# A linear-recurrence layer: the first of two triangular inversions is issued beside the projections, the first half of the scan beside the second half's operands and inversion

## The chip, the cores and the metric

One core of one Trainium2 chip runs the whole kernel. The metric is the device time of one execution in microseconds; lower is better.

## The reference, cut to what matters

The reference is a two-layer diffusion backbone: layer 0 (retention, grouped attention, a dense feed-forward part), layer 1 (differential attention and a bidirectional RWKV-7 time mixing, then eight experts of which each token takes two). The change lies in RWKV-7 of layer 1: 8 heads of 64, 256 context tokens followed by 256 latent tokens, once forward (d = 0) and once backward (d = 1). Per token and head it computes

```
decay = exp(-exp(-softplus(-(w0[d] + tanh(wd) @ w2[d])) - 0.5))
a     = sigmoid(a0[d] + ad @ a2[d]);   kd = k * (1 + (a - 1) * k_a);   kk = k * k_k / |k * k_k|
s_new = s * decay + (s @ -kk) (kk * a)^T + v kd^T          # state, 64 x 64
y     = (s if d else s_new) @ r
```

Only the latent tokens' y is used; the context half gives the state with which the latent half begins.

## The kernel before, in words

The 512 tokens are two halves (half 0 is the context, half 1 the latent tokens), each half four chunks of 64 tokens. The recurrence is done in chunked form: inside a chunk, the effect of the state's own products is a unit lower triangular system of 64 rows, whose inverse is computed ahead for all chunks, heads and both directions at once. All names below are in `layer1`.

- `project` (L842): pairs of 128 projection columns, each weight chunk split into a high and a low part (`wsplit`, L261: ScalarE writes whi, VectorE wlo) and multiplied three times; `shift` (L832) mixes neighbouring tokens. It fills rT, kT, vT, twd, adT, sgd.
- `unit_keys` (L907): kk. `prep(d, half)` (L932): decays and operands of one direction and half. It loads w2, a2 and w0 on SyncE's queue (L900, L901, L245), makes sigmoids (L946, L955), cumulated decays by matmul (L965, L966), their exponentials (L967 to L969), and writes AR and BK (L971 to L981). Its work tiles Ei, Ee, En, at, tb have one buffer each.
- `inv_blocks(half)` (L1001): the 32x32 blocks, by matmul (L1017, L1020), into Lc and Lo; a 32x32 transposition gives M (L1027). `inv_diag(half)` (L1031): 31 elimination steps of two dependent VectorE instructions each (L1042, L1044) turn N into the blocks' inverses. `inv_join(half)` (L1049): two transpositions, two rounds of small matmuls (gp L1068, wp L1077) and copies (L1060, L1082) give XF, the inverses of 64 rows.
- `chain(half)` (L1194): the scan over four chunks, both directions side by side: `prepare` (L1109; the masks are L1119), `state_in`, `solve` (needs XF, L1155), `state_out`, and for half 1 `outputs`.

Program order before: a weave of projections 8, 10, 0, 2, 14 with unit_keys, prep(0,0), prep(1,0); inv_blocks(0); a weave of prep(0,1), prep(1,1), inv_blocks(1) with inv_diag(0); the bonus products (rk, L1089 to L1097); inv_join(0); a weave of chain(0) with inv_diag(1), inv_join(1); then chain(1) with `finish`.

`weave` (L94) sets only the order in which generators issue: each counts as done in so many steps, and the one least far along goes next. The tile framework then plans each engine's queue: an instruction that is ready by its estimates may go ahead of an earlier one that is not. On the chip each engine's queue runs in the planned order. PSUM has eight banks of 128x512; `banks` (L152) says which of them each use takes in turn, and a bank is one tile tag with one buffer. A tile that takes a closed pool's place waits for the tiles that lay there.

Of the kernel before, what the change touches and what calls it, by code (L numbers as in the profile page):

```python
# [105 lines left out]
def seq(*gens):  # L106
    for g in gens:
        yield from g
# [8 lines left out]
def drain(g):  # L117
    for _ in g:
        pass
# [9 lines left out]
def _build(top, tc, nc, V, S, G, T, I, O):  # L129
    cp = top.enter_context(tc.tile_pool(name="const", bufs=1))  # L130
    st = top.enter_context(tc.tile_pool(name="st", bufs=4))
    cur = {}
# [19 lines left out]
    def banks(**by_use):  # L152

        use.update(by_use)

    def bank(kind):
# [2 lines left out]
            n = use[kind][turn[kind] % len(use[kind])]  # L159
            return ps.tile([128, 512], F32, name=name, tag=f"b{n}")  # L160
        return take
    acc, tpp, att, ybank = (bank(k) for k in ("acc", "tp", "at", "y"))
    banks(acc=range(6), tp=(6, 7))
    cur["re"] = cur["ce"] = ExitStack()
    top.callback(lambda: [cur[k].close() for k in ("we", "xe", "me", "he", "re", "ce", "pe")])
# [630 lines left out]
    def layer1():  # L796
# [185 lines left out]
            yield  # L982

        operands(qA, 0)
        banks(at=(3, 4, 5))
        weave((seq(*(project(i) for i in (8, 10, 0, 2, 14))), 15), (seq(unit_keys(), prep(0, 0), prep(1, 0)), 20))
        for k in ("we", "xe", "he"):
            cur[k].close()
        eB = ExitStack()
        qB = eB.enter_context(tc.tile_pool(name="rwb", bufs=1, side="right", reuse_waits="tile"))  # L990
        operands(qB, 1)
        eI = ExitStack()
        qI = eI.enter_context(tc.tile_pool(name="rwi", bufs=1, side="right", reuse_waits="tile"))
        XF = [(qI, qB)[i].tile([128, 2, 4, 4, 64], F32, name=f"XF{i}") for i in range(2)]
        for half in range(2):
            G.memset(XF[half], 0.0)
        bn = lambda name: qI.tile([128, 32, 32], F32, name=name, tag="bn", bufs=5)
        flat = lambda x: x.rearrange("p a b -> p (a b)")
        iv = {}

        def inv_blocks(half):  # L1001

            Lc = bn("Lc")
            off = acc("off")
            for d in range(2):
                dg = acc("dg")
                for c in range(4):
                    for p in range(4):
                        cp_ = slice((c * 4 + p) * 32, (c * 4 + p) * 32 + 32)
                        for x in range(2):  # L1010
                            for h in range(2):
                                hs = slice(64 * h, 64 * h + 64)
                                A = lambda i: AR[d, half][hs, p, c, 32 * i:32 * i + 32]
                                B = lambda i: BK[d, half][hs, p, c, 0, 32 * i:32 * i + 32]
                                o_ = 64 * h + 32 * x
                                l_, r_ = (A(x), B(x)) if d == 0 else (B(x), A(x))
                                T.matmul(dg[o_:o_ + 32, cp_], l_, r_, start=True, stop=True,  # L1017
                                         tile_position=(64 * h, o_))
                                if x == d:
                                    T.matmul(off[o_:o_ + 32, cp_], B(d), A(1 - d), start=True, stop=True,  # L1020
                                             tile_position=(64 * h, o_))
                S.activation(flat(Lc[:, 16 * d:16 * d + 16]), dg, AF.Copy)
                yield
            Lo = qI.tile([128, 16, 32], F32, name="Lo", tag="Lo", bufs=1)
            S.activation(flat(Lo), off, AF.Copy)
            M = bn("M")
            V.transpose(M.rearrange("p r c -> p c r"), Lc.rearrange("p u c -> p c u"))  # L1027
            iv[half] = M, Lo
            yield
# [19 lines left out]
        def inv_join(half):  # L1049

            N, Lo = iv[half]
            X0, X1 = bn("X0"), bn("X1")
            V.transpose(X0.rearrange("p u c -> p c u"), N.rearrange("p r c -> p c r"))
            V.transpose(X1.rearrange("p u r -> p r u"), N)
            yield
            xf, xt = (X0, X1), (X1, X0)
            xF = XF[half].rearrange("p d c a t -> p d (c a) t")
            for d in range(2):
                for x in range(4):
                    (S.copy if x % 2 else V.tensor_copy)(xF[32 * x:32 * x + 32, d, :, 32 * (x % 2):32 * (x % 2) + 32],  # L1060
                                                         xt[d][32 * x:32 * x + 32, 16 * d:16 * d + 16])
            gp = acc("gp")
            Gs = qI.tile([128, 16, 32], F32, name="Gs", tag="Gs", bufs=1)
            for d in range(2):
                for u in range(16):
                    for h in range(2):
                        i_, o_ = 64 * h + 32 * d, 64 * h + 32 * (1 - d)
                        T.matmul(gp[o_:o_ + 32, u * 32:u * 32 + 32], Lo[i_:i_ + 32, u], xf[d][i_:i_ + 32, 16 * d + u],  # L1068
                                 start=True, stop=True, tile_position=(i_, o_))
            S.activation(flat(Gs), gp, AF.Copy)  # L1070
            yield
            wp_ = acc("wp")
            for d in range(2):
                for u in range(16):
                    for h in range(2):
                        o_, i_ = 64 * h + 32 * d, 64 * h + 32 * (1 - d)
                        T.matmul(wp_[o_:o_ + 32, u * 32:u * 32 + 32], Gs[i_:i_ + 32, u], xt[d][i_:i_ + 32, 16 * d + u],  # L1077
                                 start=True, stop=True, tile_position=(i_, o_))
            for d in range(2):
                for h in range(2):  # L1080
                    o_ = 64 * h + 32 * d
                    S.activation(xF[o_:o_ + 32, d, :, 32 * (1 - d):32 * (1 - d) + 32],  # L1082
                                 wp_[o_:o_ + 32].rearrange("p (u t) -> p u t", u=16), AF.Copy)
            yield

        banks(acc=(3, 4, 5), at=(0, 1, 2))
        drain(inv_blocks(0))
        weave((seq(prep(0, 1), prep(1, 1), inv_blocks(1)), 19), (inv_diag(0), 32))
        rk = q.tile([128, 4, 256], F32, name="rkT", tag="Ei", bufs=1)  # L1089
        for p in range(4):  # L1090
            V.scalar_tensor_tensor(rk[:, p], rT[:, p], vcol("rk", p), kT[:, p, 256:512], op0=ALU.mult, op1=ALU.mult)
        hind = rc("hind").rearrange("p (a b) -> p a b", a=4)
        for b in range(2):
            t = tpp()
            for p in range(4):
                T.matmul(t[:, 0:8], rk[:, p, b * 128:(b + 1) * 128], hind[:, p], start=(p == 0), stop=(p == 3))
            V.tensor_copy(bon[:, b], t[:, 0:8])  # L1097
        banks(acc=range(6))
        drain(inv_join(0))
        eT.close()  # L1100

        def chain_pool():
            return top_pool("chain")

        eC, q = chain_pool()
        St, Y, ops, zs = {}, {}, {}, {}
        heads = [(p, h, slice(64 * h, 64 * h + 64)) for p in range(4) for h in range(2)]

        def prepare(d, half, c):  # L1109

            bk, ar = BK[d, half], AR[d, half]
            gc, w = half * 4 + c, 64 * (1 + half)
            Lm = q.tile([128, 8, 128], F32, name="Lm", tag="Lm", bufs=4)
            a = [acc("lm") for h in range(2)]
            for p, h, hs in heads:
                T.matmul(a[h][:, p * w:(p + 1) * w], bk[hs, p, c].rearrange("p a t -> p (a t)"), ar[hs, p, c, 0:w],
# [4 lines left out]
            t = tpp()  # L1121
            for p in range(4):
                T.transpose(t[:, p * 128:(p + 1) * 128], bk[:, p, c].rearrange("p a t -> p (a t)"), ident)
            bkt = q.tile([128, 512], F32, name="bkt", tag="bkt", bufs=4)
            S.activation(bkt, t, AF.Copy)
            UV = q.tile([128, 512], F32, name="UV", tag="UV", bufs=4)
            G.memset(UV[0:64], 0.0)
            t = tpp()
            for p in range(4):
# [4 lines left out]
        def state_in(d):  # L1134

            c, ar, Lm, bkt, UV = ops[d]
            S0 = St.get(d)
            z = acc("z")
            zv = z[:, 0:256].rearrange("p (a v) -> p a v", a=4)
            for p, h, hs in heads:  # L1140
                hd = 2 * p + h
                T.matmul(zv[hs, p], Lm[:, 4 * h + p, 0:64], UV[:, hd * 64:hd * 64 + 64], start=(p == 0),
                         stop=(S0 is None and p == 3), tile_position=(0, 64 * h), skip_group_check=True)
            if S0 is not None:
                for p, h, hs in heads:
                    T.matmul(zv[hs, p], ar[hs, p, c, 0:64], S0[hs, p], start=False, stop=(p == 3),
                             tile_position=(64 * h, 64 * h), skip_group_check=True)
            zs[d] = q.tile([128, 4, 64], F32, name="zs", tag="zs", bufs=2)
            (S.copy if d else V.tensor_copy)(zs[d], zv)

        def solve(d, half):
# [68 lines left out]
                ops.update(nxt)  # L1220
                yield

        weave((chain(0), 16), (seq(inv_diag(1), inv_join(1)), 32))
        eI.close()
        eC.close()
        mh, ml = (qA.tile([128, 8, 256], F32R, name=n_, tag=t_) for n_, t_ in (("mixh", "BK00"), ("mixl", "BK10")))
        G1, G2 = (qA.tile([128, 2, 512], F32, name=n_, tag=t_) for n_, t_ in (("G1", "AR00"), ("G2", "AR10")))
        cur["sb"], cur["rb"] = 2, 5
# [15 lines left out]
        def finish():  # L1244

            for b in range(2):
# [14 lines left out]
                yield  # L1261
                split_next()
                yield
        eC, q = chain_pool()
        banks(acc=range(4), y=(4, 5))
        for h in range(2):
            Y[h] = ybank("Y")
# [621 lines left out]
```

## Time and profile before

| | us |
|---|---|
| median of 3 runs | 2106.11 (2105.66 to 2109.67) |
| profiled execution | 2111.12 |
| its span | 2109.4 |
| TensorE busy in the span | 2018.4 (96%) |
| VectorE | 1637.6 (78%) |
| ScalarE | 1214.5 (58%) |

PE is TensorE's matmul stream, PEld its weight loads, DVE VectorE, ACT ScalarE, POOL GpSimd, SP SyncE, which issues most transfers. A busy PE is not a PE at its peak. PEclk is the granted TensorE clock as a share of full speed (1.0 is 2.4 GHz, 0.5 is 1.2 GHz). "L1042" is a line of the kernel before; "out<-in" are tile names; the bracket behind a row is the engine's idle time ahead of it and what ended it. RWKV-7 and its inversions take about a tenth of the span; the expert stage takes the half behind it.

### The profile page before, as it was taken

The numbers are of one execution on the slowest core, as the hardware profiler recorded it, in microseconds if no ns is written. First come the engines' busy times: TensorE is split into PE (matmuls) and PEld (weight loads), VectorE is DVE, ScalarE is ACT, GpSimd is POOL, SyncE is SP. The second block draws the span as 40 slices with busy tenths as digits, with TensorE's granted clock in tenths as the row PEclk, the third lists the DMA queues.
The fourth block names the chain that finished last, engine by engine and source line by source line (L and its number), as shares of the span: only waits on it lengthen the run. The fifth ranks groups of instructions, "written<-read, shape, count | busy, mean of one in ns | idle before, by whom it ended". The sixth has DMA issues, their size and how long they took to land. (4 is left out here: it accounts for less than half of the span.)

```text
span 2109.4 us, 30113 instructions
## 1 busy us (share of the span) xinstructions
PE 2018.4 (96%) x11649; PEld 1620.8 (77%) x11650; DVE 1637.6 (78%) x2075; ACT 1214.5 (58%) x1563; POOL 93.4 (4%) x107
## 2 busy tenths in 40 slices
PE   6999989999999899889989999999999999999997
PEld 2766778878788677778878888888888888888885
DVE  3977794675557657678578999899989899899987
ACT  3643342222235445643348878777777777777775
POOL 0211010000000110100010000000000000000000
PEclk8999999999999999977899999999999999999999
DMA  8535352476545331101187989999999999999993
GB/s 301 165 102 168 104 177 70 136 240 215 182 159 190 113 90 55 34 19 36 38 324 269 366 312 365 342 355 378 345 352 344 357 383 349 345 360 356 372 366 134
DMA packets 224202, 494.00 MB, mean 234 GB/s; under 512 B 11355, under 2 KB 45262, under 8 KB 224054
## 3 DMA queue, kind: packets, MB, share of 16 engines
q1 hardware_dynamic: 219968, 482.62, 65.1%
q10 hardware_dynamic: 4086, 9.40, 1.3%
q8 instruction: 93, 1.52, 0.3%
q14 instruction: 55, 0.45, 0.1%
HBM read 490.87 MB, written 1.11 MB: 233 GB/s over the span
## 5 line engine op out<-in xcount | busy, mean ns | idle before, releaser
L278 DVE TENSOR_TENSOR mlo<-mraw,mhi 128x1024 fp32r<-128x1024 f32 x668 | 788.6, 1222 | 74.0 <-ACT mhi L277 57.0
L277 ACT ACTIVATE mhi<-mraw 128x1024 fp32r<-128x1024 f32 x668 | 684.3, 1058 | 98.8 <-PE y L274 48.2
L267 ACT ACTIVATE whi<-raw 128x1024 fp32r<-128x1024 f32 (+1 forms) x150 | 153.1, 1025 | 274.1 <-PE acc L274 113.0
L268 DVE TENSOR_TENSOR wlo<-raw,whi 128x1024 fp32r<-128x1024 f32 (+1 forms) x146 | 173.0, 1189 | 136.4 <-ACT whi L267 136.1
L272 PE MATMUL acc<-hTh,whi 128*128 128x512 f32 (+1 forms) x504 | 191.4, 382 | 0.0
L273 PE MATMUL acc<-hTl,whi 128*128 128x512 f32 (+1 forms) x504 | 187.6, 373 | 0.0
L274 PE MATMUL acc<-hTh,wlo 128*128 128x512 f32 (+1 forms) x504 | 186.7, 371 | 0.0
L342 DVE SCALAR_TENSOR_TENSOR part<-mraw,cond,part 128x1024 f32<-128x1024 f32 x112 | 150.0, 1360 | 40.5 <-DMA mraw<-in_mod_w 40.3
L273 PE MATMUL g<-mlo,xh 128*128 128x512 f32 x448 | 180.3, 402 | 0.0
L272 PE MATMUL g<-mhi,xh 128*128 128x512 f32 x448 | 176.7, 395 | 0.0
L273 PE MATMUL y<-mlo,acts 128*128 128x512 f32 x448 | 175.6, 392 | 0.3 <-DVE mlo L278 0.3
L274 PE MATMUL g<-mhi,xl 128*128 128x512 f32 x448 | 175.2, 391 | 0.0
L273 PE MATMUL u<-mlo,xh 128*128 128x512 f32 x448 | 174.8, 390 | 0.1
L272 PE MATMUL u<-mhi,xh 128*128 128x512 f32 x448 | 174.8, 390 | 0.0
L274 PE MATMUL y<-mhi,acts 128*128 128x512 f32 x448 | 174.8, 390 | 0.0
L274 PE MATMUL u<-mhi,xl 128*128 128x512 f32 x448 | 174.4, 389 | 0.0
L272 PE MATMUL y<-mhi,acts 128*128 128x512 f32 x448 | 151.4, 390 | 0.0
L273 PE MATMUL acc<-wlo,hTh 128*128 128x512 f32 x336 | 134.3, 400 | 4.5 <-DVE wlo L268 4.5
L272 PE MATMUL acc<-whi,hTh 128*128 128x512 f32 x336 | 135.2, 405 | 3.2 <-ACT whi L267 1.9
L274 PE MATMUL acc<-whi,hTl 128*128 128x512 f32 x336 | 133.1, 397 | 0.0
L272 PEld LDWEIGHTS acc<-hTh,whi 128*128 128x128 f32 x504 | 96.3, 192 | 22.7 <-issue 4.1
L273 PEld LDWEIGHTS acc<-hTl,whi 128*128 128x128 f32 x504 | 96.4, 191 | 17.5 <-issue 2.8
(432 smaller groups left out, 3312.4 us busy)
## 6 DMA issues: line engine op xcount, KB each, us to landing
mraw<-in_moe_w_gate SPq DMA_DIRECT2D x112, 1024.0 KB
mraw<-in_moe_w_up SPq DMA_DIRECT2D x112, 1024.0 KB
mraw<-in_moe_w_down SPq DMA_DIRECT2D x110, 1024.0 KB
mraw<-in_mod_w SPq DMA_DIRECT2D x96, 512.0 KB
raw<-in_ffn_w_down SPq DMA_DIRECT2D x32, 512.0 KB
raw<-in_odd_w_in SPq DMA_DIRECT2D x26, 512.0 KB
raw<-in_even_w_in SPq DMA_DIRECT2D x24, 512.0 KB
raw<-in_ffn_w_gate SPq DMA_DIRECT2D x20, 512.0 KB
```

The lines of the kernel that those rows point to most:

```text
L267: S.activation(h, v, AF.Copy)
L268: (eng or V).tensor_tensor(l, v, h, op=ALU.subtract)
L272: T.matmul(out, ah, bh, start=first, stop=False)
L273: T.matmul(out, ah, bl, start=False, stop=False)
L274: T.matmul(out, al, bh, start=False, stop=last)
L277: S.activation(hi, src, AF.Copy)
L278: eng.tensor_tensor(lo, src, hi, op=ALU.subtract)
L342: V.scalar_tensor_tensor(part[r], w, c_, part[r], op0=ALU.mult, op1=ALU.add)
```

## The change

`inv_blocks`, `inv_diag` and `inv_join` become one generator `invert(half)`. The first weave gets `invert(0)`; the second half's `prep`, the bonus products (as `bonus()`) and `invert(1)` are woven with `chain(0)`. The inversion's pool moves to the left side and opens before the first weave; to make room the ring of split weights has two buffers there instead of four, and the inversion's five interchangeable buffers become three with fixed users. The PSUM banks are dealt anew, and Lo is copied in two pieces per direction. The pools of the decays, the inversion and the first scan stay open until the second weave ends.

```diff
-        banks(at=(3, 4, 5))
-        weave((seq(*(project(i) for i in (8, 10, 0, 2, 14))), 15), (seq(unit_keys(), prep(0, 0), prep(1, 0)), 20))
-        for k in ("we", "xe", "he"):
-            cur[k].close()
...
+        cur["we"].close()
+        open_w(2)
+        eI, qI = top_pool("rwi")
+        XF = {}
+        def inverses(half, pool):
+            XF[half] = pool.tile([128, 2, 4, 4, 64], F32, name=f"XF{half}")
             G.memset(XF[half], 0.0)
-        bn = lambda name: qI.tile([128, 32, 32], F32, name=name, tag="bn", bufs=5)
+        inverses(0, qI)
+        places = {"Lc": 0, "M": 1, "N": 0, "X0": 1, "X1": 2, "Gs": 0}
+        bn = lambda name: qI.tile([128, 32, 32], F32, name=name, tag=f"bn{places[name]}", bufs=1)
...
-            off = acc("off")
+            Lo = qI.tile([128, 16, 32], F32, name="Lo", tag="Lo", bufs=1)
             for d in range(2):
-                dg = acc("dg")
+                dg, off = ivb("dg"), ivb("off")
...
-                yield
-            Lo = qI.tile([128, 16, 32], F32, name="Lo", tag="Lo", bufs=1)
-            S.activation(flat(Lo), off, AF.Copy)
+                for o_ in (32 * d, 64 + 32 * d):
+                    S.activation(flat(Lo[o_:o_ + 32]), off[o_:o_ + 32], AF.Copy)
+                yield
...
-            gp = acc("gp")
-            Gs = qI.tile([128, 16, 32], F32, name="Gs", tag="Gs", bufs=1)
+            gp = ivb("gp")
+            Gs = bn("Gs")[:, 0:16]
...
-        banks(acc=(3, 4, 5), at=(0, 1, 2))
-        drain(inv_blocks(0))
-        weave((seq(prep(0, 1), prep(1, 1), inv_blocks(1)), 19), (inv_diag(0), 32))
...
-        banks(acc=range(6))
-        drain(inv_join(0))
-        eT.close()
+        def invert(half):
+            return seq(inv_blocks(half), inv_diag(half), inv_join(half))
...
+        banks(at=(3, 4, 5), iv=(3, 4, 5))
+        weave((seq(*(project(i) for i in (8, 10, 0, 2, 14))), 15),
+              (seq(unit_keys(), prep(0, 0), prep(1, 0), invert(0)), 62))
+        for k in ("we", "xe", "he"):
+            cur[k].close()
...
+        operands(qB, 1)
+        inverses(1, qB)
+        banks(acc=range(4), at=(4, 5), iv=(4, 5))
...
-            Lm = q.tile([128, 8, 128], F32, name="Lm", tag="Lm", bufs=4)
+            Lm = cq.tile([128, 8, w], F32, name="Lm", tag="Lm", bufs=4)
...
-        weave((chain(0), 16), (seq(inv_diag(1), inv_join(1)), 32))
+        weave((chain(0), 16), (seq(prep(0, 1), prep(1, 1), bonus(), invert(1)), 54))
+        eC.close()
         eI.close()
-        eC.close()
+        eT.close()
```

## Rows read from the trace of the kernel before

**Rows 1.** Stretches: length; busy (instructions) of PE, PEld, DVE, ACT, POOL; PEclk; DMA; GB/s
```profile
832.40:1011.00 178.60, 156.41 (x2383) 131.77 (x2381) 130.49 (x272) 82.05 (x142) 14.72 (x24) 0.81 0.13 41
...
901.50:951.40 49.90, 40.53 (x563) 35.42 (x562) 41.56 (x98) 19.26 (x32) 2.59 (x6) 0.74 0.07 20
...
965.80:996.80 31.00, 30.23 (x574) 27.33 (x574) 26.22 (x79) 9.19 (x20) 3.94 (x8) 0.88 0.07 21
```
**Rows 2.** Timeline of DVE, keys and decays of half 0: start, us, instruction, idle before
```profile
846.21 0.75 DVE L929 SCALAR_TENSOR_TENSOR kk<-kT,vec,tp 128x512 f32<-128x512 f32 x1 [0.62 <-PE tp L928]
...
858.20 0.75 DVE L929 SCALAR_TENSOR_TENSOR kk<-kT,vec,tp 128x512 f32<-128x512 f32 x1
861.35 0.69 DVE L945 TENSOR_TENSOR sgw<-tp,w0b 128x512 f32<-128x512 f32 x1 [2.40 <-DMA w0b<-in_rwkv_w]
...
873.36 1.23 DVE L972 TENSOR_TENSOR AR<-kk,Ee 128x1024 f32<-128x1024 f32 x1 [0.75 <-ACT Ee L969]
...
880.04 0.48 DVE L840 SCALAR_TENSOR_TENSOR sgd<-sh,muh,sgd 128x256 f32<-128x256 f32 x1
...
890.39 1.23 DVE L972 TENSOR_TENSOR AR<-kk,Ee 128x1024 f32<-128x1024 f32 x1
```
**Rows 3.** Groups of PE, 832.4 to 1011: records, busy us, mean ns, idle before
```profile
L965 PE MATMUL ci<-cst_rwkv,sgw 128*128 128x128 f32 x64 | 11.5, 310 | 2.4 <-ACT sgw L946 2.4
L966 PE MATMUL ce<-cst_rwkv,sgw 128*128 128x128 f32 x64 | 10.9, 294 | 2.9 <-ACT at L955 1.5 <-ACT Ei L968 1.3
...
L953 PE MATMUL la<-adT,a2p 128*128 128x256 f32 x32 | 9.6, 422 | 1.1 <-ACT at L955 1.1
...
L928 PE MATMUL tp<-knrm,spread 8*128 8x512 f32 x8 | 4.4, 654 | 0.0
```
**Rows 4.** Timeline of DVE, decays and blocks of half 1
```profile
903.37 1.23 DVE L959 SCALAR_TENSOR_TENSOR tb<-kk,at 128x1024 f32<-128x1024 f32 x1 [0.32 <-ACT at L955]
...
908.19 1.22 DVE L972 TENSOR_TENSOR AR<-kk,Ee 128x1024 f32<-128x1024 f32 x1
...
923.69 1.22 DVE L972 TENSOR_TENSOR AR<-kk,Ee 128x1024 f32<-128x1024 f32 x1
...
929.65 2.05 DVE L1027 STREAM_TRANSPOSE M<-Lc 128x1024 f32<-128x1024 f32 x1
```
**Rows 5.** Timeline of DVE, steps: half 0 from first to last, end of half 1
```profile
901.52 0.21 DVE L1042 TENSOR_TENSOR tmv<-M,N 128x31 f32<-128x31 f32 x1
...
946.38 0.36 DVE L1042 TENSOR_TENSOR tmv<-M,N 128x192 f32<-128x192 f32 x1
...
951.23 0.19 DVE L1044 TENSOR_TENSOR N<-N,tmv 128x31 f32<-128x31 f32 x1
...
997.17 0.19 DVE L1044 TENSOR_TENSOR N<-N,tmv 128x31 f32<-128x31 f32 x1
```
**Rows 6.** Groups of DVE, 832.4 to 1011: the steps of both halves
```profile
L1042 DVE TENSOR_TENSOR tmv<-M,N 128x31 f32<-128x31 f32 (+15 forms) x62 | 21.1, 340 | 1.3
L1044 DVE TENSOR_TENSOR N<-N,tmv 128x31 f32<-128x31 f32 (+15 forms) x62 | 21.0, 339 | 1.0
```
**Rows 7.** Timeline of ACT: last copies of the two joins
```profile
963.33 2.42 ACT L1082 ACTIVATE XF<-wp 32x512 f32<-32x512 f32 x4 [4.95 <-PE wp L1077]
...
1008.54 2.39 ACT L1082 ACTIVATE XF<-wp 32x512 f32<-32x512 f32 x4 [3.52 <-PE wp L1077]
```
**Rows 8.** Timeline of PE inside the first join
```profile
957.95 1.96 PE L1116 MATMUL lm<-AR,BK 64*128 64x64 f32 x8 [0.70 <-ACT Lo L1025]
```
**Rows 9.** Timeline of POOL: the memset of the second N
```profile
951.25 0.96 POOL L1035 MEMSET N<- 128x1024 f32 x1 [19.81 <-DVE tmv L1042]
```
**Rows 10.** One stretch, columns as in rows 1
```profile
936.00:972.00 36.00, 33.04 (x423) 29.83 (x424) 24.32 (x68) 11.78 (x21) 1.12 (x2) 0.50 0.08 22
```
**Rows 11.** Groups of ACT, 832.4 to 1011
```profile
L955 ACT ACTIVATE at<-la,vec 128x256 f32<-128x256 f32 x16 | 7.0, 472 | 2.6 <-PE la L953 2.5
L267 ACT ACTIVATE whi<-raw 128x1024 fp32r<-128x1024 f32 (+1 forms) x7 | 6.6, 937 | 10.2 <-PE acc L273 10.1
```

More of the change, by code (lines that the diff above doesn't have):

```diff
@@ L161, in bank @@
         return take
-    acc, tpp, att, ybank = (bank(k) for k in ("acc", "tp", "at", "y"))
+    acc, tpp, att, ybank, ivb = (bank(k) for k in ("acc", "tp", "at", "y", "iv"))
     banks(acc=range(6), tp=(6, 7))
@@ L984, in layer1 @@
         operands(qA, 0)
-        banks(at=(3, 4, 5))
-        weave((seq(*(project(i) for i in (8, 10, 0, 2, 14))), 15), (seq(unit_keys(), prep(0, 0), prep(1, 0)), 20))
-        for k in ("we", "xe", "he"):
-            cur[k].close()
[L989 to L995, printed above, removed]
+        cur["we"].close()
[4 more added lines that the diff above has]
+            XF[half] = pool.tile([128, 2, 4, 4, 64], F32, name=f"XF{half}")
             G.memset(XF[half], 0.0)
-        bn = lambda name: qI.tile([128, 32, 32], F32, name=name, tag="bn", bufs=5)
+        inverses(0, qI)
+        places = {"Lc": 0, "M": 1, "N": 0, "X0": 1, "X1": 2, "Gs": 0}
+        bn = lambda name: qI.tile([128, 32, 32], F32, name=name, tag=f"bn{places[name]}", bufs=1)
         flat = lambda x: x.rearrange("p a b -> p (a b)")
@@ L1071, in inv_join @@
             yield
-            wp_ = acc("wp")
+            wp_ = ivb("wp")
             for d in range(2):
@@ L1084, in inv_join, with bonus @@
             yield
-        banks(acc=(3, 4, 5), at=(0, 1, 2))
-        drain(inv_blocks(0))
-        weave((seq(prep(0, 1), prep(1, 1), inv_blocks(1)), 19), (inv_diag(0), 32))
[L1089 to L1094, printed above, removed]
-            for p in range(4):
-                T.matmul(t[:, 0:8], rk[:, p, b * 128:(b + 1) * 128], hind[:, p], start=(p == 0), stop=(p == 3))
-            V.tensor_copy(bon[:, b], t[:, 0:8])
-        banks(acc=range(6))
-        drain(inv_join(0))
-        eT.close()
+        def invert(half):
+            return seq(inv_blocks(half), inv_diag(half), inv_join(half))
+        def bonus():
+            rk = q.tile([128, 4, 256], F32, name="rkT", tag="Ei", bufs=1)
+            for p in range(4):
+                V.scalar_tensor_tensor(rk[:, p], rT[:, p], vcol("rk", p), kT[:, p, 256:512], op0=ALU.mult, op1=ALU.mult)
+            hind = rc("hind").rearrange("p (a b) -> p a b", a=4)
+            for b in range(2):
+                t = tpp()
+                for p in range(4):
+                    T.matmul(t[:, 0:8], rk[:, p, b * 128:(b + 1) * 128], hind[:, p], start=(p == 0), stop=(p == 3))
+                V.tensor_copy(bon[:, b], t[:, 0:8])
+            yield
[4 more added lines that the diff above has]
+            cur[k].close()
+        eB = ExitStack()
+        qB = eB.enter_context(tc.tile_pool(name="rwb", bufs=1, side="right", reuse_waits="tile"))
+        operands(qB, 1)
+        inverses(1, qB)
+        banks(acc=range(4), at=(4, 5), iv=(4, 5))
         def chain_pool():
             return top_pool("chain")
-        eC, q = chain_pool()
+        eC, cq = chain_pool()
         St, Y, ops, zs = {}, {}, {}, {}
@@ L1123, in prepare @@
                 T.transpose(t[:, p * 128:(p + 1) * 128], bk[:, p, c].rearrange("p a t -> p (a t)"), ident)
-            bkt = q.tile([128, 512], F32, name="bkt", tag="bkt", bufs=4)
+            bkt = cq.tile([128, 512], F32, name="bkt", tag="bkt", bufs=4)
             S.activation(bkt, t, AF.Copy)
-            UV = q.tile([128, 512], F32, name="UV", tag="UV", bufs=4)
+            UV = cq.tile([128, 512], F32, name="UV", tag="UV", bufs=4)
             G.memset(UV[0:64], 0.0)
@@ L1147, in state_in @@
                              tile_position=(64 * h, 64 * h), skip_group_check=True)
-            zs[d] = q.tile([128, 4, 64], F32, name="zs", tag="zs", bufs=2)
+            zs[d] = cq.tile([128, 4, 64], F32, name="zs", tag="zs", bufs=2)
             (S.copy if d else V.tensor_copy)(zs[d], zv)
@@ L1263, in finish @@
                 yield
-        eC, q = chain_pool()
+        eC, cq = chain_pool()
         banks(acc=range(4), y=(4, 5))
```

## The prediction, made before the kernel was built or run

> **What bounds the kernel now.** I read the stages first, then the engine timelines inside them, then the waits. From the first square of the keys (832.4 us) to the end of the second inversion (1011) the span holds 178.6 us, in which VectorE is busy 130.5 [rows 1]; so 48.1 us of VectorE idle time is the most that a new order of the same VectorE work could ever give back. Behind 1011 nothing is touched but where some tiles lie: the second scan, the output projection and the expert stage follow as one block, so the change is worth what it moves the end of the second inversion.
>
> Up to there the kernel before walks this chain: keys, decays of direction 0, decays of direction 1, blocks, 31 elimination steps of half 0 (901.52 to 951.42), the join (XF of half 0 complete at 963.33 + 2.42 = 965.75), the first scan beside the steps of half 1 (to 997.36), the second join (complete at 1008.54 + 2.39 = 1010.93) [rows 2, 5, 7]. The steps of half 0 last 49.9 us, in which VectorE is 83% busy [rows 1], because the decays of half 1 are taken in between: one step, one foreign instruction, and so on. The first scan's 31.0 us are full on TensorE (30.23 us) [rows 1].
>
> **The change, step by step.** No arithmetic is removed. Times below are those of the profiled execution, each step put against the same point of before.
>
> 1. *Keys.* The four products begin at 846.21 and the last at 858.20, spread out among projection matmuls [rows 2]. The second part of the first weave is now counted as 62 steps in place of 20, so the keys come before the next weights. Each product needs two matmul records of 0.654 us with overlap, 4.4 us for all four [rows 3]: three more products take 3.3 us, the last begins at 849.5, 8.7 earlier. The decay bias w0b still loads only when the tile that it shares is released; its wait (2.40 us) moves along. So the end of AR, direction 0, goes from 874.59 to 865.9.
>
> 2. *Direction 1 of half 0.* It shares its buffers with direction 0. From AR to AR it was 17.03 us behind in half 0 and 15.50 us in half 1, where it had the same priority as the rest [rows 2, 4]. I take 15.5: AR ends at 881.4 instead of 891.62. Beside it run the rest of the projections, whose last shift (sgd) VectorE did at 880.0 [rows 2].
>
> 3. *Blocks.* From AR to the end of the transposition M it took 6.8 us in half 1 and 9.9 in half 0 [rows 4, 2, 5]. I take 6.8, since TensorE comes straight from the projections here, and keep 9.9 as the other end. New: N takes the buffer of Lc, so its memset (0.96 us) [rows 9] can begin only behind M, where it lay hidden before. Start of the steps: 889.2, 12.3 earlier.
>
> 4. *Steps of half 0.* All 124 instructions of two inversions are busy 42.1 us [rows 6], 21.05 for one; where nothing came between, 16 of them took 5.04 us from 946.38 to the end [rows 5] for 4.5 us of their own, so 62 take about 23.1. What can still come between? The buffers of one tag go out in program order: on an idle GpSimd, the memset of the second N waits 19.81 us, until the last step of half 0 frees a third buffer, though two of the five were free [rows 9]. The second half's decays (la, ci, ce) now use banks 4 and 5, and by the order of calls the first join's gp has 4 and its wp has 5 ahead of them. So they can't slip in; only their four bias additions (0.69 each) [rows 2] and four scan masks do (0.4 each, an estimate from the 0.36 us of a step of 128x192 [rows 5]), 4.4 us. End: 916.7, which is 34.7 earlier.
>
> 5. *First join.* 14.33 us before [rows 5, 7]; in it eight scan matmuls of 1.96 us stood in TensorE's queue between its two products, held by a bank of the second inversion [rows 8]. That is gone: 12.4, so XF of half 0 is complete at 929.1.
>
> 6. *Decays of half 1.* They were done by then in the kernel before; now they start here. la (4 records of 0.42) and two sigmoids of 0.47 [rows 3, 11] make some 3 us, then 6.0 us from tb to AR and 15.5 to the second AR [rows 4]. On TensorE they stand beside the first scan: half of lines 953, 965 and 966 is 16.0 us [rows 3]. If the scan gives way it costs 0, if everything runs in line 16; I take 3, nearer to 0, as these matmuls come in short bursts between ScalarE's and VectorE's work. Second AR: 956.7, 31.8 later than before.
>
> 7. *Blocks of half 1.* 6.8 + 1.0 us: the steps start at 964.5. This is where most of step 4 goes back: before, M of half 1 was ready at 931.7 [rows 4].
>
> 8. *Steps of half 1.* 23.1 us, plus what is left of the scan: 929.1 + 31.0 + up to 16.0 us of foreign matmuls is 976, so 11.6 us beside it, and the scan uses a third of VectorE (26.2 us less some 16 of the steps' 21) [rows 1, 6]: 3.8 us. End: 991.4.
>
> 9. *Second join.* 13.57 us [rows 5, 7]: 1005.0 against 1010.93, a gain of 5.9 us.
>
> The small edits. The ring of split weights goes from four to two: ScalarE already waits 10.1 us for a buffer there [rows 11], a chunk of matmuls covers the next split, and I take 0; bare, each of the seven splits costs some 2 us. Lo is copied in four pieces of 32 rows (0.59 each, as line 1082's [rows 7]) behind Lc and 25 us ahead of its reader: 0. The first scan has four banks, not six; in step 5 the loss is on the old side. Loads issued on SyncE: the weights of the decays move with their step, and the output projection's are queued behind them, in buffers that come free at step 7, ahead of the second scan: 0. The second scan's buffers now lie over those of the inversion, so its first copies can't run ahead of the join; ScalarE did them behind line 1082 before too [rows 7]: 0, at most 2 us. The bonus products, four short VectorE instructions, move from beside the steps of half 0 to behind step 6, under a scan that TensorE bounds: 0.
>
> The profiled execution took 2111.1 us (span 2109.4 and 1.7 around it), 5.0 above the median of 2106.1. With 5.9 off, the median comes to 2100.
>
> **A rule weighed.** From 936 to 972, through the first join and the first scan's start, the granted clock is 0.50 (1.2 GHz) while TensorE is busy 33.04 of 36 us [rows 10]. The Trainium skill, "TensorE: Matmul & The Clock Gate", Part 1, says that the throttled rate is the default and that activity releases it; by it step 6 would find the full rate soon after the scan begins, its 3 us would vanish and the sum would be 2097. In the rows the clock stayed at its lower level through that whole stretch of work, so I don't count on it.
>
> **Rivals.**
> A, *the second half is not held.* If the decays of half 1 get through before the first join without lengthening the steps, only blocks remain behind 929.1: 936.9 + 23.1 + 10 us of scan work + 13.6 = 984, a gain of 27, 2079. For it: the kernel before does put them between the steps. Against: they did lengthen them, from 23.1 to 49.9. Half of that stretch gives 2087.
> B, *the projections lose what the inversion wins.* With a ring of two, the splits lie bare (2 us for some of the seven), direction 1's block matmuls stand behind late projection matmuls, and step 3 begins 6 us later: no change, 2106. For it: ScalarE already waits for the ring. Against: the chunk that covers it.
> C, *the second inversion is now in line behind the first, on a slow TensorE: slower.* In step 6 the clock stays at 0.50 as in [rows 10]: 16.0 us at a mean of 0.81 [rows 1] become 26, the scan's first quarter (30.2 us at 0.88) becomes 13; 39 us against the 27.5 of the sum, then 3 more for the blocks and 3 for what is left of the scan: 17.5 late, 2118; with the clock back on the way, 2115. It decides when the second AR of half 1 ends later than 962.6 (956.7 + 5.9). For it: the stage's mean clock was 0.81 and TensorE is quiet during step 4. Against: in the scan the clock did return (0.88 mean).
> That the change does not do what it says (the first inversion beside the projections) is in the sum in part: keys, decays and blocks of half 0 run beside the projections, but their steps only from 889 on, behind the last shift.
>
> **How the numbers follow.** Forecast 0.48: 2100, on its own 2092 to 2108 (3.1 us in step 3, 3 to 8 in step 6, 4 for foreign work in step 4). A 0.14 (2079 to 2090), B 0.16 (2103 to 2110), C 0.22 (2110 to 2118). With a tenth left out on each side: 2083 to 2117. Within 0.2% (2101.9 to 2110.3) is about what a measurement of this kernel can't tell from no change. Faster by more: three fifths of the forecast, all of A, little of B, 0.46; same: a third of the forecast and three fifths of B, 0.25; slower 0.29.
>
> **What would show it.** Right: the first line 1042 near 889 (past 894 under B), no second-half decays between the steps of half 0 and their last near 917, line 955 of half 1 only behind the first join, the steps of half 1 beginning near 965, the second join ending near 1005. Under A the decays of half 1 stand before 929; under C the clock is 0.50 there and the second AR comes after 962. The forecast is wrong if the steps of half 1 begin before 950 or after 972.

## The result, and the profile after

The changed kernel is slower: 2121.94 us (median of 4 runs, 2119.53 to 2125.31) against 2107.89 (4 runs, 2105.66 to 2111.08), a ratio of 1.0064, 95% interval 1.0050 to 1.0078. The forecast was 2100 (2083 to 2117): wrong in sign, and outside its range. The profiled execution took 2121.23 us, span 2119.4, 10.0 more than the span before. That is nearly all at one place: the second XF is complete at 1021.31 instead of 1010.93, and what follows only shifts. (In the changed kernel the steps are L1041 and L1043, the last copies of a join L1081.)

VectorE's timeline of the changed kernel, the rows that answer to [rows 2, 4, 5] (start, us, instruction, idle time before it and what ended it):

```profile
861.79 1.23 DVE L972 TENSOR_TENSOR AR<-kk,Ee 128x1024 f32<-128x1024 f32 x1 [0.93 <-ACT Ee L969]
...
876.36 1.22 DVE L972 TENSOR_TENSOR AR<-kk,Ee 128x1024 f32<-128x1024 f32 x1
...
884.92 2.16 DVE L1026 STREAM_TRANSPOSE M<-Lc 128x1024 f32<-128x1024 f32 x1 [3.13 <-ACT Lc L1021]
...
888.42 0.21 DVE L1041 TENSOR_TENSOR tmv<-M,N 128x31 f32<-128x31 f32 x1 [0.47 <-POOL N L1035]
...
919.81 0.19 DVE L1043 TENSOR_TENSOR N<-N,tmv 128x31 f32<-128x31 f32 x1
...
938.08 1.23 DVE L959 SCALAR_TENSOR_TENSOR tb<-kk,at 128x1024 f32<-128x1024 f32 x1 [4.41 <-ACT at L955]
...
960.28 1.22 DVE L972 TENSOR_TENSOR AR<-kk,Ee 128x1024 f32<-128x1024 f32 x1
...
972.79 2.09 DVE L1026 STREAM_TRANSPOSE M<-Lc 128x1024 f32<-128x1024 f32 x1 [0.27 <-ACT Lc L1021]
...
976.14 0.21 DVE L1041 TENSOR_TENSOR tmv<-M,N 128x31 f32<-128x31 f32 x1 [0.98 <-POOL N L1035]
979.04 0.42 DVE L1158 COPY zs<-z 128x256 f32<-128x256 f32 x1 [2.69 <-PE z L1155]
...
1008.74 0.19 DVE L1043 TENSOR_TENSOR N<-N,tmv 128x31 f32<-128x31 f32 x1
```

The two lots of steps (888 to 920 and 976 to 1009) stand apart, and all decays and blocks of half 1 lie between them. ScalarE shows why they begin where they do, and answers to [rows 7]:

```profile
930.03 2.43 ACT L1081 ACTIVATE XF<-wp 32x512 f32<-32x512 f32 x4 [3.54 <-PE wp L1076]
932.48 0.47 ACT L955 ACTIVATE at<-la,vec 128x256 f32<-128x256 f32 x1
...
963.04 0.57 ACT L1021 ACTIVATE Lc<-dg 128x512 f32<-128x512 f32 x1
...
972.16 0.60 ACT L1021 ACTIVATE Lc<-dg 128x512 f32<-128x512 f32 x1 [7.94 <-PE dg L1016]
...
1018.92 2.39 ACT L1081 ACTIVATE XF<-wp 32x512 f32<-32x512 f32 x4 [3.54 <-PE wp L1076]
```

The first sigmoid of half 1 starts 0.02 us behind the last copy of the first join, which stands ahead of it in ScalarE's own queue. TensorE's timeline has the hold itself: idle for 10.99 us ahead of the join, TensorE still begins la, which that sigmoid reads, only behind the join's second product:

```profile
922.11 3.67 PE L1067 MATMUL gp<-X,Lo 32*32 32x32 f32 x128 [10.99 <-DVE X L1052]
926.54 3.44 PE L1076 MATMUL wp<-X,Gs 32*32 32x32 f32 x128 [0.76 <-ACT Gs L1069]
929.91 1.22 PE L953 MATMUL la<-adT,a2p 128*128 128x256 f32 x2
```

That is where the bank hold named by the prediction would show; own_banks below tests it. The second Lc waits 7.94 us for the block matmuls of direction 1. What TensorE did meanwhile, by groups of 960 to 975 (records, busy us, mean ns, idle before):

```profile
L1019 PE MATMUL off<-AR,BK 64*32 64x32 f32 x128 | 4.9, 200 | 0.0
L1016 PE MATMUL dg<-AR,BK 64*32 64x32 f32 x128 | 3.7, 212 | 2.2 <-issue 1.8 <-ACT Lc L1021 0.4
L1096 PE MATMUL tp<-cst_rwkv,rkT 128*128 128x8 f32 x16 | 3.3, 313 | 0.0
```

The bonus products (L1096) stand among the blocks. The clock while the blocks of half 1 are made, in the kernel before (first row) and in the changed kernel, columns as in [rows 1]:

```profile
924.00:930.00 6.00, 4.38 (x200) 4.14 (x200) 6.00 (x10) 0.60 (x1) 0.48 (x2) 0.72 0.01 3
...
960.00:966.00 6.00, 4.65 (x308) 4.26 (x304) 6.00 (x9) 1.74 (x4) 0.99 (x2) 1.00 0.32 93
966.00:972.00 6.00, 5.16 (x122) 4.71 (x122) 1.72 (x7) 0.00 (x0) 0.00 (x0) 0.71 0.14 46
```

Stretches of the changed kernel, columns as in [rows 1]: the steps of half 0, a part of them, the end of the blocks, the steps of half 1, a part of them, and from the first square to the second XF:

```profile
888.40:920.00 31.60, 21.76 (x173) 16.74 (x171) 28.14 (x80) 11.29 (x21) 4.25 (x6) 0.90 0.04 13
912.00:918.00 6.00, 0.00 (x0) 0.00 (x0) 5.49 (x16) 0.00 (x0) 0.00 (x0) 0.66 0.00 0
...
968.00:974.00 6.00, 5.38 (x77) 4.74 (x76) 2.54 (x6) 1.20 (x2) 0.00 (x0) 0.54 0.35 88
976.10:1008.90 32.80, 19.60 (x341) 16.85 (x339) 27.94 (x82) 7.47 (x14) 0.01 (x1) 0.81 0.25 88
996.00:1008.00 12.00, 0.54 (x8) 0.35 (x6) 10.97 (x31) 0.00 (x0) 0.00 (x0) 0.64 0.00 1
832.40:1021.30 188.90, 151.88 (x2389) 124.94 (x2387) 136.25 (x277) 90.79 (x154) 14.07 (x26) 0.84 0.15 45
```

Twice TensorE and ScalarE have next to nothing to do while VectorE takes steps alone (912 to 918, and 996 to 1008); the kernel before had other work there [rows 1]. To the second XF VectorE idles 188.9 - 136.3 = 52.6 us against 48.1.

### The profile page after: what moved, and what is told of

Read it like the earlier page. It is cut to its first block, busy times and chain, and to the rows that moved or that the text cites. A ratio compares the mean times of both kernels' runs of the same rounds, so it can differ in the third digit from the quotient of the medians.

```text
span 2119.4 us, 30097 instructions
## 1 busy us (share of the span) xinstructions
PE 2017.1 (95%) x11649; PEld 1615.9 (76%) x11650; DVE 1639.3 (77%) x2075; ACT 1218.6 (57%) x1571; POOL 94.1 (4%) x107
```

## The experiments

Theory: the second inversion stands in line behind the first, held by PSUM banks, and what the early start wins (31 us at the last step of half 0) is given back there. Rivals: the ring of two and late projections; the clock; the scan's place in the queues. Each ratio is against the kernel before, run on the same chip. "Second XF" is the end of the second join in the profiled execution; single executions of one kernel differ by several us, so a milestone is weaker evidence than a ratio.

| run | median us | ratio, 95% interval | second XF |
|---|---|---|---|
| changed kernel | 2121.94 | 1.0064, 1.0050 to 1.0078 | 1021.3 |
| own_banks | 2113.92 | 1.0028, 1.0016 to 1.0041 | 1015.4 |
| own_tiles_only | 2116.13 | 1.0034, 1.0024 to 1.0045 | 1017.6 |
| own_tiles | 2105.29 | 0.9987, 0.9977 to 0.9996 | 1004.7 |
| bonus_last | 2119.99 | 1.0061, 1.0047 to 1.0074 | 1018.5 |
| own_tiles_bl | 2099.62 | 0.9959, 0.9945 to 0.9972 | 997.3 |
| best_kf | 2101.13 | 0.9970, 0.9959 to 0.9981 | 1001.2 |
| first_half | 2127.33 | 1.0088, 1.0072 to 1.0103 | 1027.1 |
| second_half | 2130.90 | 1.0109, 1.0091 to 1.0126 | 1032.6 |
| scan_first | 2133.64 | 1.0115, 1.0096 to 1.0134 | 1036.0 |
| decays_first | 2122.09 | 1.0066, 1.0052 to 1.0079 | 1023.6 |
| warm | 2126.36 | 1.0076, 1.0062 to 1.0090 | 1029.8 |
| ring_two | 2104.96 | 0.9986, 0.9977 to 0.9996 | 1003.2 |
| keys_first | 2105.03 | 0.9983, 0.9973 to 0.9994 | 1005.4 |
| ring_keys | 2106.64 | 0.9998, 0.9986 to 1.0010 | 1003.0 |

**The bank hold.**

```diff
-            gp = ivb("gp")
-            wp_ = ivb("wp")
+            gp = jnb("gp")
+            wp_ = jnb("wp")
-        banks(at=(3, 4, 5), iv=(3, 4, 5))
+        banks(at=(3, 4, 5), iv=(3, 4), jn=(5,))
-        banks(acc=range(4), at=(4, 5), iv=(4, 5))
+        banks(acc=range(3), at=(3, 4), iv=(3, 4))
```

> The changed kernel with PSUM dealt so that the first join's gp and wp share bank 5 and the decays and blocks of half 1 have banks 3 and 4 (the first scan keeps three banks). Theory (the second inversion stands in line behind the first because la of half 1 must wait for gp and wp): line 955 of half 1 starts before 910 us instead of 932.5, its tb and AR stand between the steps of half 0, which stretch from 31.6 to some 50 us (as in the kernel before), the first XF comes near 951, but the blocks of half 1 then need only some 8 us and the second XF is complete near 1002 instead of 1021.3: 2121.9 - 19 = 2103 us, about 0.2% under the kernel before. Rival (TensorE and its clock are the limit of the second weave, not the hold): the second XF stays within 4 us of 1021 and the time at 2118 to 2124. Rival (three banks for the scan cost as much as the hold gives): line 955 early, but the scan's own chain over 5 us longer, 2112 to 2118.

The hold is what it was taken for: line 955 of half 1 (L956 in this run) starts at 901 instead of 932.5, and both ARs of half 1 (916.5, 933.7) stand between the steps of half 0. But half of the expected gain stays out, and ScalarE's timeline shows where:

```profile
901.14 0.47 ACT L956 ACTIVATE at<-la,vec 128x256 f32<-128x256 f32 x1
...
954.61 0.59 ACT L1022 ACTIVATE Lc<-dg 128x512 f32<-128x512 f32 x1
...
969.78 0.60 ACT L1022 ACTIVATE Lc<-dg 128x512 f32<-128x512 f32 x1 [3.54 <-PE off L1020]
```

AR of direction 1 is written at 935.0, and M comes at 970.4: a second hold. Lc of half 1 lies in the place that N and then Gs of half 0 have, until the first join's second product has read Gs. So direction 0's block matmuls are done at 937, but their copy Lc comes at 954.61, and direction 1's block matmuls run only from 964.5 on, among the scan's. The time, 2113.9 us, lies in the range of the last rival (three banks for the scan); but own_tiles below has the same three banks and a ratio 0.41% lower, so they are not what is missing.

**The tile hold.**

```diff
-        bn = lambda name: qI.tile([128, 32, 32], F32, name=name, tag=f"bn{places[name]}", bufs=1)
+        later = {"Lc": "at", "M": "tb", "N": "En", "X0": "at", "X1": "Ee", "Gs": "tb"}
+        bn = lambda name, half=0: (q if half else qI).tile([128, 32, 32], F32, name=name, bufs=1,
+                                                           tag=later[name] if half else f"bn{places[name]}")
...
```

(Lo of half 1 goes into a tile of sgw.) Alone, with the banks as changed:

> The changed kernel with the second inversion's tiles in places of their own (work tiles of the decays), the banks as changed: la of half 1 still waits for gp and wp. Theory (two holds in a row, of which the banks are the outer one): the decays of half 1 still begin behind the first join, so M of half 1 comes only 0 to 3 us earlier (972.8 to 970), time 2118 to 2122. Rival (the places of the tiles are the hold by themselves): steps of half 1 begin before 966 and the time is 2112 or less.

The decays still begin at 933.8 and M comes at 973.3: the banks are the outer hold, as the theory has it. The time fell more than it allowed (2116.1); the second steps had less between them, 29.8 us instead of 32.8. In the changed kernel two weight splits of the output projection (wlo, 1.22 us each) stand among them; here these come behind the second join, from 1022.5 on. So a part of this run's 0.30% is not the hold. With both edits:

> The run with banks of its own for the second half, and besides that the second inversion's tiles no longer in the first one's places: Lc, M, N, X0, X1, Gs and Lo of half 1 lie in work tiles of the decays that are free once direction 1's AR and BK are written. Theory (with the bank hold gone, the tile places are the second hold: Lc of half 1 waits for N of half 0, so its blocks come behind the first join and there stand in TensorE's queue among the scan's matmuls, 19.6 us from the first XF to the second M): M of half 1 comes within 3 us of the first join's transpositions, near 947 instead of 970, the steps of half 1 run from 948 to 985 beside the join and the scan, the second XF is complete near 998 (before: 1010.9, with the banks alone: 1015.4), and the time is 2096 to 2100, 0.4 to 0.6% under the kernel before. Rival (TensorE's slow clock behind its quiet stretch holds the blocks wherever they stand): M past 960 and the time at 2108 to 2114.

```profile
945.13 2.06 DVE L1029 STREAM_TRANSPOSE M<-Lc 128x1024 f32<-128x1024 f32 x1
```

M of half 1 comes at 945.1 and the steps go from 951.4 to 992.3, beside the join and the scan. The time is below the kernel before, though 5 us above what was expected: the first join took 17.6 us (from its first transposition at 939.55 to 957.14; the expectation of own_tiles_bl below misreads it as 15.7), with bonus and block matmuls ahead of it in TensorE's queue, and the steps 40.9 instead of 37.

**The bonus products**, in the changed kernel and on top of both edits:

```diff
-        weave((chain(0), 16), (seq(prep(0, 1), prep(1, 1), bonus(), invert(1)), 54))
+        weave((chain(0), 16), (seq(prep(0, 1), prep(1, 1), invert(1), bonus()), 54))
```

> The changed kernel with the bonus products issued behind the second inversion instead of ahead of its blocks. Theory (in TensorE's queue they stand among the blocks of direction 1, whose 13.4 us from the last AR to M were 6.8 in the kernel before): AR to M falls to 8 or 9 us and the time by some 5, to 2117 us. Rival (the blocks are slow because the clock is near 0.5 there, or because TensorE has the scan's matmuls in line): AR to M stays at 12 or more and the time at 2120 to 2123.

From the second AR to the end of M it is 10.8 us instead of 13.4: half of what was expected; the ratio hardly moves. The rival's slow clock is not what is left: the granted clock was 1.00 (2.4 GHz) all through this stretch. TensorE's timeline shows scan matmuls ahead of direction 1's blocks and two gaps in which nothing in the profile holds it:

```profile
966.06 0.45 PE L1177 MATMUL s<-UV,bkt 128*64 128x64 f32 x7 [1.49 <-issue]
...
970.16 0.24 PE L1016 MATMUL dg<-AR,BK 64*32 64x32 f32 x4 [1.67 <-issue]
```

> The run with banks and tiles of its own for the second half, and the bonus products behind the second inversion. In the run before, the first join took 15.7 us against 12.5 and the bonus matmuls stood in TensorE's queue ahead of it. If they are the reason: join 12.5 to 13.5, second XF near 1001 to 1002 instead of 1004.7, 2102 to 2104 us. If it is the block matmuls of half 1 beside the join, or the clock: join 15 or more, 2104 to 2107.

Best version of all, faster than both kernels: ratio 0.9959 (0.9945 to 0.9972) to the kernel before, 2.4 us below the expectation. VectorE's timeline, and the last copy of the first join:

```profile
888.64 0.20 DVE L1044 TENSOR_TENSOR tmv<-M,N 128x31 f32<-128x31 f32 x1
...
928.29 1.22 DVE L973 TENSOR_TENSOR AR<-kk,Ee 128x1024 f32<-128x1024 f32 x1
...
934.38 0.18 DVE L1046 TENSOR_TENSOR N<-N,tmv 128x31 f32<-128x31 f32 x1
...
940.09 2.08 DVE L1029 STREAM_TRANSPOSE M<-Lc 128x1024 f32<-128x1024 f32 x1
...
942.42 0.21 DVE L1044 TENSOR_TENSOR tmv<-M,N 128x31 f32<-128x31 f32 x1
...
945.42 2.42 ACT L1084 ACTIVATE XF<-wp 32x512 f32<-32x512 f32 x4 [3.54 <-PE wp L1079]
...
984.64 0.19 DVE L1046 TENSOR_TENSOR N<-N,tmv 128x31 f32<-128x31 f32 x1
```

Between the two lots of steps lie 7.9 us instead of 56.1, and the first join is back at 13.0 us (934.9 to 947.8). The bonus products need not be the whole difference to own_tiles: the clock in the first 5 to 6 us of the join is 0.78 here and 0.50 there. The second lot starts before the first join is done.

own_tiles alone has the ratio of two small edits to the kernel before (0.9986 and 0.9983, ring_two and keys_first below): with both holds gone the loss is undone, but a gain beyond such edits shows only with the bonus products behind. The kernel before with nothing but its bonus products moved was not run, so how much of the 0.41% that this run gains is theirs alone is open.

**One half of the change alone.** First the early inversion without the scan beside the decays, then the reverse:

```diff
+        drain(seq(prep(0, 1), prep(1, 1), bonus(), inv_blocks(1)))
+        weave((chain(0), 16), (seq(inv_diag(1), inv_join(1)), 32))
```

> The changed kernel with only its first half: the first inversion in the first weave, but the decays of half 1, the bonus products and the blocks of half 1 drained ahead of the weave of the first scan with the steps and join of half 1. The bank hold stays. Theory (13 of the 10 lost us come from the hold, the rest from the scan's matmuls and VectorE work in the way of decays, blocks and steps): first XF near 932, second AR near 958 instead of 961.5, its M some 8 us behind instead of 13.4, steps of half 1 from 968 beside the whole scan, second XF near 1015, 2116 us. Rival (without the scan beside them nothing is won, since the scan then lies bare): 2121 to 2126. Rival (the scan is the whole loss): second XF at 1008 or less, 2107 to 2110.

```diff
-              (seq(unit_keys(), prep(0, 0), prep(1, 0), invert(0)), 62))
+              (seq(unit_keys(), prep(0, 0), prep(1, 0)), 20))
+        drain(invert(0))
```

> The changed kernel with only its second half: the first weave weighs as before (20) and ends without the inversion, which is drained behind it; decays, blocks and steps of half 1 stay beside the first scan. Theory (the halves add: the first is worth some 6 to 13 us, the second costs more): steps of half 0 begin near 898 to 902, last near 925, first XF near 938, and from there the same 88.9 us as in the changed kernel: second XF near 1027, 2125 to 2128 us. Rival (the late projections of the changed kernel are its loss): the steps of half 0 stand alone here, 23 us, and the time is under 2118.

first_half went past its first rival: the theory took the scan's matmuls for a part of the slow blocks, and without them AR to the end of M took 15.5 us. But the clock was 0.62 on average there, against 0.76 in the changed kernel, so this run does not part the scan from the clock. second_half went the way of the theory and 3 us past its range: second XF 11.3 us later than with both halves. Its rival expected the steps of half 0 to stand alone, 23 us; the last shift was ahead of them, and they still took 29.1, 3.4 of them waits of two bias additions for TensorE. So the early start is worth that much, and putting decays and second inversion behind the first costs over 20.

**The order of scan and decays** (16 in the changed kernel):

```diff
-        weave((chain(0), 16), ...
+        weave((chain(0), 48), ...    # scan_first
+        weave((chain(0), 6), ...     # decays_first
```

> The changed kernel with one number changed: the first scan counts as 48 steps in its weave instead of 16, so its instructions go ahead of the second half's decays. Theory (the decays and the scan share VectorE's and TensorE's queues, whichever goes first): the scan's last state comes near 978 instead of 996, the decays' second AR near 968 instead of 961.5, the steps of half 1 start near 980 and then stand almost alone (25 us instead of 32.8), second XF within 4 us of 1021, 2117 to 2123. Rival (the scan's rest between the steps of half 1 is a loss by itself): second XF at 1014 or less, 2112 to 2115.

Both missed: the scan's last state came 10 us earlier, but the second AR 18.6 later, and the time went up. VectorE's timeline:

```profile
978.87 1.22 DVE L972 TENSOR_TENSOR AR<-kk,Ee 128x1024 f32<-128x1024 f32 x1
...
998.78 0.20 DVE L1041 TENSOR_TENSOR tmv<-M,N 128x31 f32<-128x31 f32 x1
...
1022.95 0.19 DVE L1043 TENSOR_TENSOR N<-N,tmv 128x31 f32<-128x31 f32 x1
```

The steps then took 24.4 us, near the 23.1 that the prediction had for steps alone: what they lose in the changed kernel is the scan's VectorE work, one more weight split and waits for the scan's matmuls. But the scan is only cover; the decays are the path.

> The changed kernel with one number changed: the first scan counts as 6 steps in its weave instead of 16, so the second half's decays and blocks go ahead of it. Theory (the decays of half 1, not the scan, are the path to the end; bringing the scan forward cost 15 us at the second XF): the second AR near 958 instead of 961.5, M of half 1 near 970 instead of 972.8, the scan ends later but still ahead of the last step; second XF near 1017 instead of 1021.3, 2117 to 2119 us. Rival (the given order was already the best and the scan then lies bare behind the steps): 2121 us or more.

The rival's time came, though not its reason: the scan's last state is written at 1003.8, ahead of the last step at 1011.2, and M came at 975.0 instead of 970. With both holds in place neither of these two orders helps.

**The clock.**

```diff
+                if t >= 12:
+                    r_ = min(n * m, 128)
+                    T.matmul(warm()[0:r_, 0:256], tm[:, 0:r_], kk[:, 0, 0:256], start=True, stop=True)
```

> The changed kernel with added matmuls that nobody reads: behind each of the last 19 steps of either inversion one of 256 columns into bank 3, which waits for the step's product (the scan keeps three banks). They fill TensorE's idle stretches 912 to 920 and 996 to 1009, behind which the clock was 0.50. Theory (the lost time is order, not clock): if the clock stays at 1.00 there, each join falls from 12.4 to some 11 and the first decays behind it start 1 us earlier, 3 to 4 us in all, 2117 to 2119. Rival (C of the prediction in another place: the slow clock behind TensorE's idle stretch is the loss): joins of 9 to 10, blocks of half 1 at 9 us instead of 13.4, 2112 or less. If the clock falls in spite of them: 2120 to 2124.

Stretches, columns as in [rows 1]:

```profile
912.00:918.00 6.00, 6.00 (x44) 4.50 (x43) 5.40 (x14) 3.01 (x5) 0.52 (x1) 1.00 0.21 66
918.00:924.00 6.00, 5.46 (x18) 2.60 (x17) 5.01 (x14) 0.00 (x0) 0.00 (x0) 1.00 0.01 3
924.00:930.00 6.00, 4.49 (x52) 1.93 (x54) 5.28 (x13) 0.63 (x2) 0.00 (x0) 1.00 0.01 1
930.00:936.00 6.00, 5.00 (x188) 4.73 (x184) 2.35 (x5) 2.43 (x4) 0.00 (x0) 0.50 0.01 3
936.00:942.00 6.00, 6.00 (x76) 4.64 (x71) 0.83 (x2) 3.51 (x7) 0.00 (x0) 0.50 0.01 3
```

Beside the added matmuls the clock stayed at 1.00 (2.4 GHz) from 912 to the end of the steps, which became 2.3 us longer. Then, with TensorE busy 5.00 of 6 us in the join's 32x32 matmuls, it fell to 0.50 (1.2 GHz) all the same. The run is slower, 2.4 us more than said for that case. It does not tell what a join at the full clock would take; that stays open. On the blocks of half 1 it does tell something: with the clock at 0.90 on average from the second AR to M, against 0.81 in the changed kernel, AR to the end of M took 13.1 us against 13.4, not the rival's 9.

**The ring and the weights**, in the kernel before:

```diff
+        cur["we"].close()
+        open_w(2)                                                    # ring_two, ring_keys
-    ... (seq(unit_keys(), prep(0, 0), prep(1, 0)), 20))
+    ... (seq(unit_keys(), prep(0, 0), prep(1, 0)), 62))              # keys_first, ring_keys
```

> The kernel before with one edit, the ring of split weights at two buffers instead of four from the first weave on. If the ring of two is what made the projections late (last shift sgd 897.8 instead of 880.0) and lengthened the steps of half 0: last shift past 885 and the time 2 to 5 us above the kernel before, 2110 to 2113. If the lateness came only from the new priority of keys and decays: last shift within 3 us of 880 and no change, 2107 to 2109.

> The kernel before with one number changed: in the first weave the second part (keys, decays of half 0) counts as 62 steps instead of 20, as in the changed kernel. Theory (the early start of the first inversion is real and is lost only behind it): steps of half 0 begin near 889 to 892 instead of 901.5, everything behind keeps its length, the second XF is complete near 1000 to 1002 instead of 1010.9, and the time falls by 8 to 10 us to about 2099. Rival (what the keys win, the later projections lose, since the operands of half 1 need rT and the split weights take VectorE's time between the steps): second XF within 3 us of 1011, 2105 to 2109.

> The kernel before with the two edits that each made it a little faster alone: the ring of two and the weight 62 for keys and decays in the first weave; bank deal, interleaving of the second half's decays with the steps of half 0, and the rest as before. If they add: steps of half 0 from 890, second XF near 998, 2100 to 2102 us. If both do the same thing (they let keys and decays go ahead of weight splits on ScalarE and VectorE): as one alone, second XF near 1003 and 2103 to 2106 us.

The ring of two costs nothing: last shift at 881.3, and the time 0.14% below (0.04 to 0.23%). The weight 62 alone gains as little: last shift at 887.2, steps of half 0 from 896.2. Together they do not add: no difference. In the profiled executions all three have the second XF 5 to 8 us earlier than the kernel before; their medians say 1 to 4 us. The steps begin no earlier than 895.8, because projections stand in front of them; only with the inversion in the first weave is it 888 to 893.

**What is left in the best version.** Its first weave counted as 40 instead of 62:

> The run with banks and tiles of its own and the bonus products last, and the first weave's second part counted as 40 steps instead of 62. If the projections' rest between the first steps (31.6 instead of 27.5 us in the changed kernel) is part of the loss: steps of half 0 begin 2 to 4 us later than 888.6 but have less between them, M of half 1 is planned ahead of the first join, second XF at 993 to 995 instead of 997.3, 2096 to 2099 us. If it is only a trade: second XF 997 to 1000, 2099 to 2103 us.

A trade: M of half 1 came at 941.1, ahead of the first join, but the steps of half 0 began at 893.0 and the first join ended 9.4 us later, at 957.2.

## Why the prediction was wrong

Steps 1 to 3 held in their sum, first steps at 888.4 (forecast 889.2), and that was partly luck: the two ARs of half 0 ended 2.9 and 3.8 us ahead of the forecast, and the blocks behind them took 10.8 us instead of 7.8. Step 5 held: first join 12.5 us (12.4). The ring at no cost held (ring_two). The bank hold held: no la of half 1 between the steps of half 0, line 955 right behind the join (own_banks took it away). Rival C's place was right, the second inversion in line behind the first; its mechanism was not: the clock, 0.50 up to 936, was back at 1.00 from 942 on, sooner than the forecast counted on, and the second AR came at 961.5, short of the 962.6 from which it was to decide.

The second XF was 16.3 us later than forecast; the terms that make it up:

- Step 4, +4.1 us: 31.6 us instead of 27.5, 8.5 foreign instead of 4.4. The rest of the projections (three wlo and the shifts up to sgd at 897.8) and the scan's first masks stand between the steps. With an earlier first inversion the last shift is no longer ahead of them; the sum had left it at 880. The projections are not all of it: second_half, without them between its steps, took 29.1 us.
- Step 6, +1.4 us, a small miss: TensorE's share was within its bounds.
- Step 7, +6.8 us, the largest: 14.6 us instead of 7.8. The 6.8 us was taken from the kernel before, where the block matmuls of direction 1 began as soon as AR was written and had TensorE's queue to themselves, 3.3 us in all. Here they begin 2.2 us behind AR, released by the copy of direction 0's Lc, and take 8.4 us: 3.3 us of bonus products, costed at 0, stand among them (bonus_last: 2.6 us less without them, with the clock at 1.00), and 1.8 us are gaps in issue. The clock is not the difference: its mean from AR to the end of M is 0.75 in the kernel before and 0.76 here. Of the scan's matmuls TensorE has only 0.8 us between AR and the end of these blocks.
- Step 8, +5.9 us: 32.8 us instead of 26.9. The sum let the scan end at 976; it ended at 996, as in the kernel before, since half of its chunks wait behind the decays in VectorE's queue. So the steps take 9.7 us more than alone, not 3.8 (scan_first: 24.4 us without the scan): 18 instructions of the scan stand between them, two weight splits of the output projection (2.4 us, which the sum had at 0 among the small edits), and 3.4 us of waits for the scan's matmuls.
- Steps 1 to 3 (-0.8) and 9 (-1.2) give a little back.

The failed step is thus 7 with 8: the sum saw that the second inversion would stand in line and charged that line with durations from a kernel in which it did not stand in line. Its own range, 2092 to 2108, had width for steps 3, 4 and 6 and none for these two. Rival A, at 0.14, is not borne out either: with both holds freed the decays do pass before the first join, but the steps of half 0 then last 47.1 us (own_tiles) and 45.9 (own_tiles_bl), the very thing named against it, and its 2079 to 2090 was not reached. What the runs add is that there are two holds, not one: with one of them freed M of half 1 came at 970.4 (banks) and 973.3 (places), with both at 945.1. Freed together they give 0.77% (1.0064 to 0.9987), the banks alone 0.36%, the tile places alone 0.30%; the bonus products, worth 0.03% with the holds in place, another 0.28% without them.

## What to carry to other kernels

Where two long chains of dependent work are to overlap, list every buffer that the second takes over from the first, PSUM banks and work tiles alike: one remaining hold keeps the chains in line, and work moved out of the first is then only added to the second. Take durations for a moved stage from a row in which its neighbours are the ones it will have. Tiles that die inside the second chain (here the decays' own) are the places for what follows in it.

## What the runs showed of the hardware

- The clock fell to 0.50 within a join of 32x32 matmuls directly behind 18 us at 1.00 (warm). The Trainium skill, "TensorE: Matmul & The Clock Gate", Part 1, has activity release the throttled rate; a TensorE that was 5.00 of 6 us busy with small matmuls did not keep it here.
- Long lots of 64x32 matmuls show gaps in which TensorE waits for nothing the profile shows: 0.91 and 0.84 us in the changed kernel, 1.67 in bonus_last (and 1.49 just behind such a lot), 1.95 in first_half, runs with quite different neighbours. During the 1.67 and the 1.95 us the DMA engines were idle (busy share 0.00). The blocks of direction 1 of half 1 in the kernel before have no such gap. What they are stays open.
